# A hybrid encoder layer on one core: 16 more tokens by gathered expert rows, activations weighted and split for two expert blocks at a time

## The chip, the cores and the metric

The kernel runs on one core of a Trainium2 chip. The metric is the device time of one execution in microseconds, as the median of several runs. The engines of the core work side by side and are tied by semaphores: TensorE (PE, matrix products; its weight loads are shown as PEld), VectorE (DVE), ScalarE (ACT), GpSimd (POOL, which here mostly issues gathers) and SyncE (SP, which issues the other transfers, in order).

## The reference

One layer of an encoder over 512 tokens of width 1024. An RMSNorm and one input projection feed an attention branch and a bidirectional state-space branch (S5, followed by a gated linear unit); both are gated, merged and projected out. Then comes the part that takes most of the time, a layer of 16384 single-neuron experts: each token has 8 heads, each head picks 16 experts by product keys (two lists of 128 keys), and the token's output is the gated sum over its 128 experts. A last RMSNorm ends it.

```python
def peer(h, w_query, sub_keys, w_down, w_up):
    ...
    scores = jnp.einsum('thnd,hnkd->thnk', q, sub_keys).astype(jnp.float32)
    s_top, i_top = lax.top_k(scores, PEER_TOPK)
    ...
    best, pos = lax.top_k(cand, PEER_TOPK)
    idx = jnp.take_along_axis(cand_idx, pos, axis=-1)
    gate = jax.nn.softmax(best, axis=-1)
    ...
    u = w_down[ib]
    act = jax.nn.gelu(jnp.einsum('cd,chkd->chk', xb, u).astype(jnp.float32)) * gb
    v = w_up[ib]
    return jnp.einsum('chk,chkd->cd', act.astype(v.dtype), v)
```

## The kernel before

**Numbers.** fp32 weights and activations are split into two fp16 halves (hi and lo), and a product is three fp16 matmuls: hi·hi, lo·hi, hi·lo. ACT makes the hi half of a weight tile, DVE the lo half (`halves`, L453 and L456 for experts; `Stream.hi` and `Stream.lo`, L485 and L493, for the other weights). `Stream` loads the other weights in a fixed order into three raw buffers (`wr`), each 128x1024.

**Front.** ACT squares the eight 128x512 pieces of x (L694). After each, four fp32 matmuls with a single column add its squares over the partitions (L696). Four square roots (L700), a reciprocal (L703) and a spread over partitions (L563, L572) lead to the first normed piece (`h_of`, L710) and the first projection (`pu`, L725 to L727). Then follow the S5 branch, attention, and from about 288 to 345 us the attention projection (`w_oa`), the GLU (`w_glu`) and the S5 output (`w_os`), whose weights come through `Stream`.

**Experts.** Two ways are used for the experts. Of the 512 tokens, 384 (tiles 1 to 3) are dense: every expert is computed for them, in 128 blocks of 128 experts. `ph1(i)` is the down projection of block i: 24 matmuls of 384 columns (L541 to L543) into a bank, then the gelu on ACT (L1479) into a slot of 128x384. There are 13 slots in the memory `area` and 35 in a ring. `ph2(i)` is the up projection: DVE multiplies the slot with the block's gates `Gb` (L1501), ACT rounds the product to fp16 `ph` (L1502), DVE makes the rest `pl` (L1503), and 18 matmuls of 512 columns (L1514 to L1516) add to six PSUM sums `ya` (three token tiles by two halves of the width). The other 128 tokens (tile 0) are gathered: for each of their 128 experts an indirect DMA fetches one row of `w_down` per token (128 rows of 4 KB), DVE reduces it against h (`gdown`, L1552), and later a row of `w_up` is weighted and added (`gup`, L1560). These are 256 gathers on ten row buffers.

**Gates.** Before ph2 the dense tokens' gates must stand as a matrix over experts. The one-hot stage makes it in 24 subtiles of 16 tokens: DVE builds one-hot factors (`ej` L1427, `eg` L1429 and L1431), PE multiplies them (L1442), ACT copies the result into a staging tile `stg` (L1444), and every 64 tokens 4 MB go to DRAM (`gd`). `gload` reads a block's gates back, 192 KB in pieces of 64 floats.

**Order.** `experts()` lists units and runs them in a row. The ph1 units come first while slots last (between the top-k of tiles 1 to 3, and within the one-hot stage), then ph2(0) and so on, with one ph1 between two ph2 while there are any, and at the end only ph2. The weights of a unit are prepared three units ahead. At the start of the pair part DVE does the top-k of tile 0. After that `gather_init` fills the list of gathers, and a planner paces them: `tp` adds up PE's cost of the units, `td` DVE's cost, and while `td` is less than `E.lead` ahead and `room` allows (it grows by `E.gcap` = 1.42 per unit), one row is worked off and one more is fetched (L1545). What is left ten units before the end is done at once. Then follow the last sums, final norm and store.

## Time and profile before

| | before |
|---|---|
| median of 3 runs | 1563.29 us (1563.12 to 1567.69) |
| profiled execution: its own time | 1559.74 us |
| profiled execution: span | 1558.0 us, 26141 instructions |
| PE busy | 1502.0 us (96%), 9921 matmuls |
| DVE busy | 1296.7 us (83%) |
| ACT busy | 742.9 us (48%) |
| POOL busy | 374.5 us (24%) |
| moved | 378.64 MB, mean 243 GB/s |

The span runs from the first to the last instruction; the execution's own time is a little longer. Busy shares are means over stages that have different limits, so a stretch is looked at by itself: first which engine is busy throughout in it, then what the others wait for. A matmul's own duration overlaps the next one's, so the distance from start to start is what one costs. "Engine time" of transfers is time on the core's 16 DMA engines; a share of 1.00 or more means that all 16 had something in hand.

### The profile page before, as it was taken

To read this page: it belongs to the slowest core of one execution; us is meant where nothing else is said; L and a number is where in the kernel's file an instruction comes from. 1 tells how busy PE (TensorE), PEld (TensorE's weight loads), DVE (VectorE), ACT (ScalarE), POOL (GpSimd) and SP (SyncE) were. 2 spreads that over 40 slices of the span, in tenths; PEclk is the share of its full clock that TensorE was granted. 3 is DMA by queue.
4 is the path that set the end of the run, shared out by engine and by line. 5 is a ranking of instruction groups with operands and counts; after the bars stand their busy time and mean duration, and the time that the engine had idled before them with its cause. 6 is when DMAs were issued, how large, how long until landed. Compare 5 with 4: busy or idle time off the path is not lost. (4 is left out here: it accounts for less than half of the span.)

```text
span 1558.0 us, 26141 instructions
## 1 busy us (share of the span) xinstructions
PE 1502.0 (96%) x9921; PEld 854.9 (55%) x9921; DVE 1296.7 (83%) x2571; ACT 742.9 (48%) x1117; POOL 374.5 (24%) x300
## 2 busy tenths in 40 slices
PE   8999999889989999999999999999999999999997
PEld 5547665448676567664444555555555555554433
DVE  4889688555999999986987988888888888888886
ACT  5456765554345479883432443333333333333334
POOL 0100100000000000000026654444555445444310
PEclk9999999999999999999999999999999999999999
DMA  5532622764103347769669999999999999999984
GB/s 192 129 97 49 94 69 90 238 201 157 42 15 125 125 140 284 277 252 332 177 218 389 385 385 366 349 347 348 367 344 354 348 345 368 351 311 323 324 270 147
DMA packets 201135, 378.64 MB, mean 243 GB/s; under 512 B 112305, under 2 KB 117809, under 8 KB 199985
## 3 DMA queue, kind: packets, MB, share of 16 engines
q1 hardware_dynamic: 159904, 231.50, 44.5%
q0 software_dynamic: 39520, 142.59, 26.9%
q10 hardware_dynamic: 1584, 2.88, 0.6%
q8 instruction: 77, 1.26, 0.3%
q14 instruction: 50, 0.40, 0.1%
HBM read 340.25 MB, written 36.14 MB: 242 GB/s over the span
## 5 line engine op out<-in xcount | busy, mean ns | idle before, releaser
L456 DVE SCALAR_TENSOR_TENSOR wlo<-raw,whi 128x1024 f16<-128x1024 f32 x256 | 311.9, 1220 | 125.3 <-ACT whi L453 124.2
L453 ACT ACTIVATE whi<-raw 128x1024 f16<-128x1024 f32 x256 | 262.0, 1050 | 168.7 <-DMA raw<-w_up 94.6
L1514 PE MATMUL ya<-whi,ph 128*128 128x512 f16 x768 | 291.9, 380 | 8.1 <-ACT ph L1502 6.1
L1515 PE MATMUL ya<-wlo,ph 128*128 128x512 f16 x768 | 291.8, 380 | 2.9 <-DVE wlo L456 2.6
L1516 PE MATMUL ya<-whi,pl 128*128 128x512 f16 x768 | 291.8, 380 | 1.0
L1545 POOL DMA_INDIRECT row<-w_dn,gidx x78 | 104.7, 1342 | 625.4 <-ACT whi L453 537.2
L543 PEld LDWEIGHTS <-wlo 128*128 128x128 f16 x1272 | 124.6, 98 | 111.7 <-DVE wlo L493 9.9
L541 PEld LDWEIGHTS <-whi 128*128 128x128 f16 x1272 | 124.6, 98 | 105.1 <-ACT whi L485 11.3
L542 PEld LDWEIGHTS <-whi 128*128 128x128 f16 x1272 | 124.6, 98 | 91.3 <-issue 1.3
L1502 ACT ACTIVATE ph<-Gb 128x384 f16<-128x384 f32 x128 | 66.5, 520 | 214.9 <-DVE Gb L1501 195.7
L1545 POOL DMA_INDIRECT row<-w_up,gidx x78 | 107.5, 1378 | 122.0 <-DVE area L1560 96.5
L1516 PEld LDWEIGHTS <-pl 128*128 128x128 f16 x768 | 75.3, 98 | 101.3 <-DVE pl L1503 11.7
L541 PE MATMUL rps<-hhl,whi 128*128 128x384 f16 x384 | 125.6, 327 | 2.6 <-ACT whi L453 2.6
L543 PE MATMUL rps<-hhl,wlo 128*128 128x384 f16 x384 | 125.9, 328 | 2.0 <-DVE wlo L456 2.0
L1514 PEld LDWEIGHTS <-ph 128*128 128x128 f16 x768 | 75.3, 98 | 94.4 <-ACT ph L1502 10.2
L542 PE MATMUL rps<-hhl,whi 128*128 128x384 f16 x384 | 125.6, 327 | 0.0
L1515 PEld LDWEIGHTS <-ph 128*128 128x128 f16 x768 | 75.3, 98 | 87.7 <-issue 2.6
L1444 ACT COPY stg<-rps 128x512 f32<-128x512 f32 x96 | 98.3, 1077 | 16.4 <-PE rps L1442 15.7
L543 PE MATMUL rota<-hhl,wlo 128*128 128x384 f16 x320 | 104.3, 326 | 1.4 <-DVE wlo L456 1.4
L541 PE MATMUL rota<-hhl,whi 128*128 128x384 f16 x320 | 104.3, 326 | 0.0
L542 PE MATMUL rota<-hhl,whi 128*128 128x384 f16 x320 | 104.3, 326 | 0.0
L541 PE MATMUL rotb<-hhl,whi 128*128 128x384 f16 x320 | 104.3, 326 | 0.0
(370 smaller groups left out, 2994.4 us busy)
## 6 DMA issues: line engine op xcount, KB each, us to landing
raw<-w_dnT SPq DMA_DIRECT2D x128, 512.0 KB
raw<-w_up SPq DMA_DIRECT2D x128, 512.0 KB
gd<-stg SPq DMA_DIRECT2D x6, 4096.0 KB
Gb<-gd SPq DMA_DIRECT2D x128, 192.0 KB
raw<-w_g SPq DMA_DIRECT2D x16, 512.0 KB
raw<-w_out SPq DMA_DIRECT2D x8, 512.0 KB
raw<-w_query SPq DMA_DIRECT2D x8, 512.0 KB
x<-x SPq DMA_DIRECT2D x8, 512.0 KB
```

The source lines that it names most:

```text
L453: E.nc.scalar.activation(hi, raw, AF.Copy, scale=scale)
L456: E.nc.vector.scalar_tensor_tensor(lo, raw, scale, hi, op0=OP.mult, op1=OP.subtract)
L541: E.nc.tensor.matmul(o, lhsT=lh, rhs=rh, start=start and i == 0, stop=False)
L542: E.nc.tensor.matmul(o, lhsT=lh, rhs=rl, start=False, stop=False)
L543: E.nc.tensor.matmul(o, lhsT=ll, rhs=rh, start=False, stop=stop and i == n - 1)
L1444: nc.scalar.copy(self.stg[:, :, t0:t0 + TQ].rearrange("p i t -> p t i"), o)
L1502: hi, lo = halves(E, wp, raw, D, "up", 3, SU, lambda: nc.scalar.activation(ph, P, AF.Copy, scale=scale))
L1514: nc.tensor.matmul(o, lhsT=ph[:, ts], rhs=hi[:, ns], start=f, stop=False)
L1515: nc.tensor.matmul(o, lhsT=ph[:, ts], rhs=lo[:, ns], start=False, stop=False)
L1516: nc.tensor.matmul(o, lhsT=pl[:, ts], rhs=hi[:, ns], start=False, stop=l)
L1545: E.nc.gpsimd.indirect_dma_start(out=r, out_offset=None, in_=E.a[src], in_offset=bass.IndirectOffsetOnAxis(ap=E.gidx[:, k:k + 1], axis=0))
```

## The change

1. **16 tokens more by gathers.** Of the 384 dense tokens the last 16 are gathered instead (`TX`, `TN` = 368). ph1's matmuls and the gelu cover 368 columns; the last 16 columns of the slots are zeroed once by GpSimd, so that ph2 still covers 384. The one-hot stage has 23 subtiles. The 16 tokens have 128 experts each, 2048 rows; they are laid on 128 partitions as 16 tokens by 8 heads, with 16 experts each. So they take 16 more gathers per weight (32 in all, 288 instead of 256). Their results (`yx`) are summed over the 8 partitions of a token by two fp32 matmuls with `sel` that add to `ya` (`extra`).
2. **Two blocks at a time.** The slots and the gates come in pairs: the product, the rounding to fp16 and the remainder are made once per two blocks of 384 (at even ph2 units), and a gate load brings two blocks (384 KB in pieces of 128 floats).
3. **Buffers and pace.** Eight row buffers instead of ten (`NX` = 4), a ring of 17 pairs and 6 pairs in `area` (46 slots instead of 48). The planner's numbers change: a ph1 unit costs DVE 1.25 instead of 1.14, a ph2 unit 3.15 or 1.25 instead of 2.2, a row 1.29 instead of 1.2, and `E.gcap` is 1.68.
4. **Front.** DVE adds the squares, then four matmuls instead of 32, one square root instead of four; the hi halves of the first two weight tiles stand ahead of the root.
5. **Wider weight buffer.** From the attention projection's stage to the end of `w_os`, `Stream` has seven raw buffers in memory that the S5 part has left.

```diff
+TX = 16
...
+    def widen(self, pool, last):
+
+        self.wide, self.end = pool, self.at[last] + 1
...
-            r = self.pool.tile([128, 1024], F32, name="raw", tag="wraw", bufs=self.bufs)
+            pool, bufs = (self.wide, 7) if i < self.end else (self.pool, self.bufs)
+            r = pool.tile([128, 1024], F32, name="raw", tag="wraw", bufs=bufs)
...
-            sso = [ps.tile([128, 1], F32, name="pss", tag="ps") for _ in range(4)]
             for k in range(KT):
                 nc.scalar.activation(sq[:, k], xT[:, k], AF.Square)
-                for c in range(4):
-                    nc.tensor.matmul(sso[c], lhsT=sq[:, k, c * 128:c * 128 + 128], rhs=E.ones[:, 0:1],
-                                     start=(k == 0), stop=(k == KT - 1))
+                if k:
+                    V.tensor_add(sq[:, 0], sq[:, 0], sq[:, k])
+            sso = ps.tile([128, 4], F32, name="pss", tag="ps")
+            for c in range(4):
+                nc.tensor.matmul(sso[:, c:c + 1], lhsT=sq[:, 0, c * 128:c * 128 + 128], rhs=E.ones[:, 0:1],
+                                 start=True, stop=True)
+            st.hi()
+            st.hi()
...
+            nc.scalar.activation(ssx, sso, AF.Sqrt, scale=1.0 / D, bias=E.eps)
...
+            w2c = ExitStack()
+            st.widen(w2c.enter_context(E.pool(name="w2", bufs=1)), "os7")
...
     TD = T - 128
+    TN = TD - TX
...
-    NX = 6
+    NX = 4
...
+        for x in self.ring:
+            self.E.nc.gpsimd.memset(x[:, :, self.TN:], 0.0)
+        self.E.nc.gpsimd.memset(self.area, 0.0)
...
+        E.dma(self.xi, E.xidx.rearrange("a (r s) -> (a r) s", s=16))
+        E.dma(self.xg, E.xgate.rearrange("a (r s) -> (a r) s", s=16))
+        E.dma(self.hx, E.xh[:, None, :].to_broadcast([TX, 8, D]))
+        E.dma(self.sel, E.a["sel"])
...
-            P = self.G[i]
-            V.tensor_tensor(P, self.slot(i), P, op=OP.mult)
-            hi, lo = halves(E, wp, raw, D, "up", 3, SU, lambda: nc.scalar.activation(ph, P, AF.Copy, scale=scale))
-            V.scalar_tensor_tensor(pl, P, scale, ph, op0=OP.mult, op1=OP.subtract)
+            if i % 2:
+                hi, lo = halves(E, wp, raw, D, "up", 3, SU)
+            else:
+                G, R = self.G[i // 2], self.pair(i // 2)
...
+                V.tensor_tensor(byc(R), byc(R), G, op=OP.mult)
+                hi, lo = halves(E, wp, raw, D, "up", 3, SU,
+                                lambda: nc.scalar.activation(self.ph, R, AF.Copy, scale=scale))
+                V.scalar_tensor_tensor(self.pl, R, scale, self.ph, op0=OP.mult, op1=OP.subtract)
...
+    def extra(self):
+
+        for n in range(2):
+            ns = slice(n * 512, n * 512 + 512)
+            self.E.nc.tensor.matmul(self.ya[2][n], lhsT=self.sel, rhs=self.yx[:, ns], start=False, stop=False)
...
-    E.lead, E.gcap = 1.0, 1.42
+    E.lead, E.gcap = 1.0, 1.68
```

How the program's order of instructions changes is shown at three places. The first is DVE at the very start, before:

```order
L1869 MEMSET ones 128x128
L1871 MEMSET eps 128x1
L703 RECIPROCAL ssx<-ssx 128x4
L563 TENSOR_TENSOR dgs<-ident,ssx 128x512
L493 SCALAR_TENSOR_TENSOR wlo<-raw,whi 128x1024
```

and after:

```order
L1930 MEMSET ones 128x128
L1932 MEMSET eps 128x1
L705 TENSOR_TENSOR sqx<-sqx 128x512 x7
L713 RECIPROCAL ssx<-ssx 128x4
L573 TENSOR_TENSOR dgs<-ident,ssx 128x512
L503 SCALAR_TENSOR_TENSOR wlo<-raw,whi 128x1024
```

The seven adds of the squares now stand on DVE ahead of the reciprocal; they are what PE's 28 further sums were.

The second is SP's queue of loads for the attention projection's stage (`w_oa`, with `w_out` and `w_query` for later stages between them), before:

```order
L1860 DMA raw<-w_out 128x1024
L1860 DMA raw<-w_oa 128x512
L1860 DMA raw<-w_query 128x1024
L1860 DMA raw<-w_oa 128x512
L1860 DMA raw<-w_query 128x1024
L1860 DMA raw<-w_oa 128x512
```

and after:

```order
L1921 DMA raw<-w_query 128x1024 x4
L1921 DMA raw<-w_oa 128x512
L1921 DMA raw<-w_query 128x1024
L1921 DMA raw<-w_oa 128x512
L1921 DMA raw<-w_glu 128x512 x2
```

With more buffers open, four loads of `w_query` come in a row ahead of the last two of `w_oa`, and `w_glu` follows at once.

The third is DVE in the pair part, before (the `ISA` rows are `gdown` and the reading of its sum; `area,gco` is `gup`):

```order
L1560 SCALAR_TENSOR_TENSOR area<-area,gco 128x1024
L1501 TENSOR_TENSOR Gb<-ring_5625,Gb 128x384
L456 SCALAR_TENSOR_TENSOR wlo<-raw,whi 128x1024
L1503 SCALAR_TENSOR_TENSOR pl<-Gb,ph 128x384
L1552 ISA area,gact<-area,h_2654 128x1024
L1552 ISA gact 128x1
L1560 SCALAR_TENSOR_TENSOR area<-area,gco 128x1024
L456 SCALAR_TENSOR_TENSOR wlo<-raw,whi 128x1024
L1552 ISA row_8331,gact<-row_8331,h_2654 128x1024
L1552 ISA gact 128x1
L1501 TENSOR_TENSOR Gb<-ring_5626,Gb 128x384
```

and after:

```order
L1549 TENSOR_TENSOR ring_5601<-ring_5601,Gb 128x6x2x64
L460 SCALAR_TENSOR_TENSOR wlo<-raw,whi 128x1024
L1552 SCALAR_TENSOR_TENSOR pl<-ring_5601,ph 128x768
L460 SCALAR_TENSOR_TENSOR wlo<-raw,whi 128x1024
L1614 SCALAR_TENSOR_TENSOR yx<-row_8210,gco,yx 128x1024
L1606 ISA area,gact<-area,h_2630 128x1024
L1606 ISA gact 128x1
L460 SCALAR_TENSOR_TENSOR wlo<-raw,whi 128x1024
L1614 SCALAR_TENSOR_TENSOR yx<-area,gco,yx 128x1024
L1606 ISA area,gact<-area,h_2630 128x1024
L1606 ISA gact 128x1
L460 SCALAR_TENSOR_TENSOR wlo<-raw,whi 128x1024
```

The product and the remainder are now of twice the width and come once in four `wlo` instead of once in two; between two `wlo` stand up to two steps of gathered rows.

## Rows read from the trace of the kernel before

**Rows 1.** The page: busy us (share of the span) and instructions by engine.
```profile
PE 1502.0 (96%) x9921; PEld 854.9 (55%) x9921; DVE 1296.7 (83%) x2571; ACT 742.9 (48%) x1117; POOL 374.5 (24%) x300
```

**Rows 2.** Timeline of the front (start, duration, instruction), and a 128x512 add.
```profile
8.40 3.30 ACT L694 ACTIVATE sqx<-xTs 128x512 f32<-128x512 f32 x5 [1.48 <-DMA xTs<-xT]
...
18.59 0.18 DVE L703 RECIPROCAL ssx<-ssx 128x4 f32<-128x4 f32 x1 [17.56 <-ACT ssx L700]
...
11.71 6.54 PE L696 MATMUL pss<-ones,sqx 128*128 128x1 f32 x30
...
L1267 DVE TENSOR_TENSOR zm<-zm,mixed 128x512 f32<-128x512 f32 x8 | 5.5, 692 | 0.3
```

**Rows 3.** Busy by engine, clock, DMA share, GB/s; then waits (total, times, longest).
```profile
288.00:345.00 57.00, 46.62 (x195) 17.72 (x194) 33.40 (x45) 30.14 (x47) 0.00 (x0) 0.97 0.67 208
...
PE pp L541 <- ACT whi L485: 6.4, 6, 2.0
```

**Rows 4.** Timeline of DVE, one period of the one-hot stage.
```profile
599.60 2.48 DVE L1431 TENSOR_TENSOR eg<-eg,ghl 128x2048 f16<-128x2048 f16 x2
602.01 1.22 DVE L456 SCALAR_TENSOR_TENSOR wlo<-raw,whi 128x1024 f16<-128x1024 f32 x1
603.14 1.22 DVE L1427 TENSOR_TENSOR ej<-iom,gij 128x2048 f16<-128x2048 f16 x1
...
605.53 2.48 DVE L1431 TENSOR_TENSOR eg<-eg,ghl 128x2048 f16<-128x2048 f16 x2
```

**Rows 5.** Timeline of PE, one pair: 24 matmuls of ph1, 18 of ph2.
```profile
1004.16 0.33 PE L541 MATMUL rota<-hhl,whi 128*128 128x384 f16 x1
...
1008.06 0.38 PE L1514 MATMUL ya<-whi,ph 128*128 128x512 f16 x1
...
1011.95 0.33 PE L541 MATMUL rotb<-hhl,whi 128*128 128x384 f16 x1
```

**Rows 6.** Busy of PE, PEld, DVE, ACT, POOL by stretch, clock, DMA share, GB/s.
```profile
860.00:1000.00 140.00, 140.00 (x757) 73.90 (x756) 124.88 (x159) 54.02 (x75) 77.62 (x54) 1.00 1.04 372
1000.00:1400.00 400.00, 400.00 (x2158) 211.01 (x2157) 341.39 (x430) 150.79 (x212) 198.73 (x147) 1.00 1.00 349
1405.00:1551.00 146.00, 139.94 (x632) 60.16 (x630) 120.88 (x163) 56.13 (x84) 34.88 (x27) 1.00 0.85 272
```

**Rows 7.** Chain that ended last, burst and tail: start, duration, what.
```profile
828.60 19.57 DMA raw<-w_up
...
1432.41 7.20 DMA raw<-w_up
```

**Rows 8.** Groups by line (count, busy, mean ns): a clear on GpSimd, the fp32 scores.
```profile
masks.py:197 POOL MEMSET ident<- 128x128 f32 x1 | 0.2, 206 | 0.3 <-POOLq L1898 0.3
...
L911 PE MATMUL pS<-KT,QT 96*128 96x512 f32 x64 | 33.2, 641 | 0.7 <-ACT KT L897 0.7
```

**Rows 9.** Timeline of DVE in the pairs (start, duration, instruction).
```profile
855.70 1.28 DVE L1560 SCALAR_TENSOR_TENSOR area<-area,gco 128x1024 f32<-128x1024 f32 x1
856.90 0.55 DVE L1501 TENSOR_TENSOR Gb<-ring,Gb 128x384 f32<-128x384 f32 x1
857.37 1.21 DVE L456 SCALAR_TENSOR_TENSOR wlo<-raw,whi 128x1024 f16<-128x1024 f32 x1
```

**Rows 10.** Transfers: 860 to 920, then 1000 to 1200, then 1420 to 1500.
```profile
DMA packets 12454, 23.07 MB, mean 385 GB/s; under 512 B 7234, under 2 KB 7234, under 8 KB 12449
...
DMA packets 37974, 70.33 MB, mean 352 GB/s; under 512 B 22065, under 2 KB 22065, under 8 KB 37960
...
q0 software_dynamic: 10508, 38.25, 53.4%
q1 hardware_dynamic: 27452, 31.90, 46.4%
...
DMA packets 19768, 26.14 MB, mean 327 GB/s; under 512 B 14227, under 2 KB 14227, under 8 KB 19762
...
q1 hardware_dynamic: 16315, 13.52, 52.7%
```

## What the change does to the time: the prediction

> **What bounds the kernel now.** First the page's busy shares [rows 1]: TensorE (PE) is busy 96% of the span, VectorE (DVE) 83%. So time can be won where PE has less to do, or in the few stretches in which it waits. A table of busy time by stretch, laid over the stages, then tells who sets the pace of each:
> - first norm: the reciprocal starts at 18.59, 6.9 after the last square, and everything waits for it [rows 2];
> - 288 to 345 (attention projection, GLU, S5 output): PE works 46.62 of 57 us; its waits end on the ACT half-split of weights that arrive by `Stream` [rows 3];
> - one-hot stage, 550 to 696: DVE works without a gap, a period of 5.93 us [rows 4];
> - pairs of a ph1 and a ph2 unit, 860 to 1405: PE is 100% busy, DVE 85 to 89%, the transfer engines at a share of 1.00 to 1.04 [rows 5, 6]. This is a third of the kernel;
> - gather burst, around 804 to 860: ten gathers go out at once, and one load of weights takes 19.57 us [rows 7];
> - tail, 1405 to 1551: only ph2; loads of w_up take 7 us and more of the chain behind gathered rows [rows 6, 7].
>
> **Front.** Before, ACT's squares end at 11.70, but PE's 64 records of sums (32 fp32 matmuls of one column, two records each; the last 30 take from 11.71 to 18.25) go on, and four square roots wait for them, one behind the other [rows 2]. Now DVE adds the squares as they come, seven adds of 0.69 (the 128x512 add of [rows 2]), about the 0.66 between two squares, so the last ends near 12.6. Four sums of one column remain, eight records, 0.22 apart by 6.54/30: 14.3. A root over 4 columns, 0.3 as other small steps, then the reciprocal starts at 14.7 instead of 18.59: **−3.9**. The two half-splits of u0 and u1 now stand ahead of the root on ACT; the squares end at 11.70, so they fit beside PE's sums if their weights have landed, which the order of the loads suggests. Bounds −2 to −4.5.
>
> **Wider weight buffer.** From the time the S5 memory is free (284 to 288) until os7 the stream holds seven raw buffers instead of three. That takes away nothing but waits for transfers. PE is idle 10.4 of the 57 us, 6.4 of it in waits for ACT's half-split, six times [rows 3]; the rest are dependencies (sigmoid, mixing) that stay. The DMA share there is 0.67, so there is room to load ahead. I take **−6**, with 0 and −10.4 as ends. What speaks against: SP issues in order, and three w_query loads now stand ahead of the last two w_oa loads; if w_oa then comes late, ACT waits for it as before.
>
> **Token index copies, memsets.** topk of tile 3 gets one more DVE instruction of 128 wide; its copies to DRAM are off the path. GpSimd clears the rings and the area. Its memset of 128x128 took 0.206 [rows 8]; if that is all columns, 5120 of them and 17 clears of 32 are 9 us, and less if a fixed part is in it. If ACT's first gelu waits for that it does so while DVE sets the pace. **+0.3**, end +4.
>
> **One-hot stage.** 23 subtiles of 16 tokens instead of 24. A subtile is, on DVE, two compares (1.14 each) and two products (2.48 for both): 4.80 from one to the next without the wlo of 1.13 that belongs to the ph1 unit beside it [rows 4]. n1 falls from 48 to 46, so two units' wlo leave as well: 4.80 + 2×1.13 = 7.06. **−7.0**, as long as DVE sets the pace. The two ph1 units come back in the pair part.
>
> **Transition.** Before the first ph2, SP gets four loads (indices, gates, a 512 KB broadcast of h, sel) ahead of Gb and w_up, but Gb comes in pairs in 512-byte instead of 256-byte pieces. +1 and −2; I take **−1**, ends −3 and +3.
>
> **Pairs: PE.** A 384-column matmul starts 0.1625 after the one before (24 take 3.90 us), a 512-column one 0.216 after (18 take 3.89): 7.79 a pair [rows 5]. 368 columns are no row of before; the nearest are 384 and 512, which both give 0.42 ns a column, so 0.1557 is an estimate and a ph1 unit 3.74. ph2 stays, as its 18 matmuls cover 128 tokens whether or not 16 are zero. The two units moved here cost 2×3.74: **+7.5**. The other 80 pairs: 7.63 at PE's pace, −0.16 each, −12.8 in all, if DVE and transfers allow it. The two extra fp32 matmuls of 512 columns, two records each, are like the fp32 scores, whose records are busy 0.641 each, overlap and all [rows 8]: at most 2.6, of which I take two thirds: **+1.7**.
>
> **Pairs: DVE.** Before: two wlo (1.13 by [rows 4]), P and pl (0.47 each, 384 wide) and 2.82 gathered rows (up to 1.20) [rows 9], 2.26+0.94+3.38 = 6.58; the row of 1000 to 1400 gives 341/400×7.79 = 6.65 [rows 6]. After: P and pl come once for two blocks, 768 wide. By the line from 384 (0.55 busy) to 1024 (1.21) that is 0.95, so 0.87 for each pair of units instead of 0.94; the four-dimensional order of P is seen in no row, end: twice 0.47, no gain. The gathered rows rise to 288 in all, paced at 13 per 8 units: 3.25 a pair, 3.90 us. Sum 7.03 of 7.63, or 92%. From 860 to 1000 DVE was busy 124.88 of 140 us, 89%, with PE at 140.00 [rows 6], so 92% is likely affordable. But each wlo that PE needs stands behind up to one row more.
>
> **Pairs: transfers.** A pair moves 524 KB for w_dnT, 524 for w_up, 197 of Gb and 524 per gathered row: before 1.245+2.82×0.524 = 2.72 MB, in 7.79 us 350 GB/s, which is just what the row of 1000 to 1400 shows (349). So there the need sets the rate. After: 1.245+3.25×0.524 = 2.95 MB; in 7.63 us 386 GB/s. From 860 to 920 the chip moved 23.07 MB, 385 GB/s, with 256-byte Gb pieces [rows 10] and with PE busy throughout [rows 6]. At that rate a pair takes 7.66: **−10.4** for 80 pairs (80×0.13). If only the steady 352 of [rows 10] were to be had, 2.95/0.352 = 8.38, +0.75 a pair against PE's pace. The engines' time says how tight it is. Let q1's 256-byte packets take a each and its large ones b a MB: the 200 us from 1000 give 22065a + 26.25b = 0.464×16×200, the 80 us from 1420 give 14227a + 9.88b = 0.527×16×80 [rows 10]; so a is 19.5 ns and b 40 us. A gathered row takes 23.4 us of engines' time (53.4% of 3200 us for 38.25 MB). After, a pair needs 42 for weights, 384 pieces of Gb at 19.5 to 39 ns, 7.5 to 15, and 3.25×23.4 = 76: 126 to 133 us on 16 engines, 7.9 to 8.3 at a share of 1.00. At the share of 1.04 that stood from 860 to 1000 [rows 6] it is 7.6 to 8.0. I take 7.66, the value of the rate that was seen while PE was not held back.
>
> The Trainium skill (page "DMA: Bandwidth & Descriptors", section "Specifications") puts the HBM limit of one NeuronCore at about 358 GB/s: by it a pair could not be under 2.95/0.358 = 8.24 us, and the change would lose about 36 us on the 80 pairs (an estimate from that page's figure). The trace disagrees: 385 GB/s for 60 us. The same section names 512 B as the least transfer at line rate; by it the Gb pieces would leave the slow kind and stand at the low end, which no run here shows yet.
>
> **Burst and tail.** Eight row buffers instead of ten let fewer gathers run ahead, but they are asked for faster: **0**, −5 to +3 by what a longer or shorter wait of that 19.57 us [rows 7] could do. In the tail PE does 630×0.216 = 136 us of work in 146: 10 lost, mostly waits for w_up [rows 6, 7]. It asks for 10 rows per 8 units instead of 11.4 and for Gb in half the packets. By the same a and b (21 us for weights, 15 for Gb before and 7.5 to 15 after, 11.4/8 rows of 23.4 before and 10/8 after) a unit's time on 16 engines falls from 4.3 to between 3.6 and 4.1, against PE's 3.9: **−4**, ends 0 and −8.
>
> **Sum.** −3.9 −6 +0.3 −7 −1 +7.5 +1.7 −10.4 +0 −4 = −22.8; I take back 2 for PE's waits on a fuller DVE: −20.8. Against the profiled execution's own 1559.74 (span 1558.0): 1538.9. The median is 1563.29, 0.23% above it, and the forecast of the median is 1563.29/1559.74×1538.9 = 1542.5.
>
> **Rivals.**
> - B, the pairs stay where they were: DVE's and the transfers' fuller queues hold a pair near 7.79. The −10.4 is gone: about 1553. For it: shares over 1.00. Against: PE at 140.00 of 140 from 860 to 1000.
> - D, the wide buffer and the earlier roots bring nothing: w_oa comes behind w_query on SP, and the clears on GpSimd hold up the first gelus. −6 and −3 or so gone, +2 more: about 1554. For it: ACT's waits there are for several tensors; against: a DMA share of 0.67.
> - C, slower: the transfers cannot go above the steady 352 GB/s over hundreds of us (HBM reads of scattered rows), and a pair takes 8.38 instead of 7.66: 80×0.72 = 58 us more, about 1600. It decides from a pair of 7.92 us, that is 372 GB/s, where the whole gain of 20.8 is spent. The limit on the Trainium skill's page above would make this case the true one. Against it: 385 GB/s from 860 to 920, and 372 from 860 to 1000 with PE at 140.00 of 140 [rows 6, 10].
>
> **How the numbers follow.** Forecast 0.58, B 0.17, D 0.15, C 0.10. Forecast's own range, from the ends of its terms: 1528 to 1552. The range reaches to B and D with some of their own width: 1528 to 1562, and leaves out C and a little. Within 0.3% (1558.6 to 1568.0; about what a measurement here tells from no change) lie the worse ends of B and D: 0.07. Slower is C: 0.10. Faster 0.83.
>
> **What would show it.** Reciprocal near 14.7; PE busy over 50 of 55 us in the oa stage; 23 subtiles at 5.93; ph1 matmuls 0.156 apart; pairs at 7.66 with a rate near 385 GB/s and PE busy throughout. I am wrong if PE has waits for w_up or w_dnT all through the pairs (C), or if matmuls of 368 columns start as far apart as those of 384 (then −10.4 is gone).

## The result, and the profile after

| | before | after |
|---|---|---|
| median | 1564.32 us (4 runs) | 1547.59 us (1544.27 to 1549.59, 4 runs) |
| ratio | | 0.9887, 95% interval 0.9864 to 0.9911 |
| profiled execution, span | 1558.0 us | 1545.6 us |

The changed kernel is faster by 1.1%, 16.7 us in the medians. The forecast was 1542.5, its own range 1528 to 1552. The time came out 5 us above the forecast, but the way to it was another one: two terms failed, a third was mis-sized, the pairs gave more than forecast, and one number that the change does not touch turned out to be worth as much as the whole change (the third buffer, below).

The page of the changed kernel, first lines (busy us, share of the span, instructions):

```profile
span 1545.6 us, 25606 instructions
...
PE 1472.6 (95%) x9837; PEld 844.0 (55%) x9837; DVE 1330.7 (86%) x2496; ACT 724.8 (47%) x1047; POOL 461.3 (30%) x352
```

Against [rows 1], PE has 29 us less to do and the span is 12.4 shorter: PE waits more than before. Where, is read by laying both timelines beside each other. The table takes the start of the first or last instruction of a kind in both traces and the difference between them; a step in the last column is what that stretch gave.

| mark | before | after | difference | step |
|---|---|---|---|---|
| last gate projection matmul (`pg`) | 288.15 | 284.03 | −4.1 | −4.1 |
| first `w_query` matmul | 380.17 | 371.22 | −8.9 | −4.8 |
| first one-hot `ej` | 549.82 | 545.72 | −4.1 | **+4.8** |
| last `stg` copy | 695.48 | 684.60 | −10.9 | −6.8 |
| first ph1 matmul of the pairs | 777.82 | 765.76 | −12.1 | −1.2 |
| last ph1 matmul of the pairs | 1404.94 | 1392.86 | −12.1 | 0.0 |
| last ph2 matmul | 1550.89 | 1538.41 | −12.5 | −0.4 |

Two ph1 and two ph2 units more lie between the marks of the pairs (82 and 81 instead of 80 and 79), one ph2 unit less before them and one less behind.

The marks are of one trace each, and a step moves by itself from trace to trace. From the last `pg` to the first `w_query` matmul the ten traces with the changed code there took 84.4 to 89.8 us (87.2 in the table's), those with the old code 92.0 and 93.1. The one-hot stage repeats within 0.1 us. The tail took 141.8 to 145.6 us in the five traces with the same code there; the table has the longest of them.

The front, timeline (start, duration, instruction):

```profile
7.45 2.64 ACT L703 ACTIVATE sqx<-xTs 128x512 f32<-128x512 f32 x4 [1.33 <-DMA xTs<-xT]
...
8.12 3.88 DVE L705 TENSOR_TENSOR sqx<-sqx 128x512 f32<-128x512 f32 x5 [1.27 <-ACT sqx L703]
14.25 0.18 DVE L713 RECIPROCAL ssx<-ssx 128x4 f32<-128x4 f32 x1 [2.25 <-ACT ssx L712]
...
13.95 0.26 ACT L712 ACTIVATE ssx<-pss,eps 128x4 f32<-128x4 f32 x1 [1.23 <-PE pss L708]
14.12 1.05 ACT L495 ACTIVATE u1hi<-raw 128x1024 f16<-128x1024 f32 x1
...
12.05 1.87 PE L708 MATMUL pss<-ones,sqx 128*128 128x1 f32 x8 [12.05 <-DVE sqx L705]
```

The adds follow the squares, four sums take 1.87 and the reciprocal starts at 14.25 instead of 18.59 [rows 2]. Of the two half-splits that the section on the change puts ahead of the root, only the first stands there (at 11.67): the kernel has one `st.hi()` in that place, not two, and the second (`u1hi`) follows the root.

PE in one pair, timeline:

```profile
1015.65 0.32 PE L551 MATMUL rota<-hhl,whi 128*128 128x368 f16 x1
1015.81 0.32 PE L552 MATMUL rota<-hhl,whi 128*128 128x368 f16 x1
...
1019.39 0.38 PE L1564 MATMUL ya<-whi,ph 128*128 128x512 f16 x1
...
1023.28 0.32 PE L551 MATMUL rotb<-hhl,whi 128*128 128x368 f16 x1
```

A pair takes 7.63 instead of 7.79 [rows 5]; 24 matmuls of 368 columns take 3.74. From 893.65 on every pair takes just that: PE sets the pace. The stretches answer to [rows 6] (busy of PE, PEld, DVE, ACT, POOL, then clock, DMA share, GB/s):

```profile
860.00:1000.00 140.00, 140.00 (x771) 75.13 (x770) 132.85 (x152) 52.89 (x68) 89.79 (x61) 1.00 1.04 397
1000.00:1400.00 400.00, 400.00 (x2202) 215.23 (x2201) 368.62 (x417) 148.31 (x188) 255.46 (x170) 1.00 1.02 388
1393.00:1539.00 146.00, 139.01 (x618) 60.64 (x615) 114.26 (x125) 52.20 (x68) 38.31 (x25) 0.98 0.77 261
```

The transfers run at 388 to 397 GB/s over 540 us, DVE is busy 92 to 95%, and PE does not wait in them. In the tail it does: 612 matmuls of ph2 instead of 630, and the same 146 us.

### The profile page after: what moved, and what is told of

Its sections match the earlier page's. It is cut to its first block, busy times and chain, and to the rows that moved or that the text cites. A ratio compares the mean times of both kernels' runs of the same rounds, so it can differ in the third digit from the quotient of the medians.

```text
span 1545.6 us, 25606 instructions
## 1 busy us (share of the span) xinstructions
PE 1472.6 (95%) x9837; PEld 844.0 (55%) x9837; DVE 1330.7 (86%) x2496; ACT 724.8 (47%) x1047; POOL 461.3 (30%) x352
## 4 chain that ended last, share of the span: by engine, by line
PE 54%; DVE 22%; issue 11%; DMA 8%; ACT 4%; POOL 1%; SPq 0%; ACTq 0%; DVEq 0%; POOLq 0%
PE ya L1566 6%; PE ya L1564 6%; PE ya L1565 6%; DMA raw<-w_up 5%; DVE wlo L460 4%; PE rotb L552 3%; PE rota L552 3%; PE rota L551 3%; PE rotb L551 3%; PE rotb L553 3%; PE rota L553 3%; PE pg L551 1%; PE pg L552 1%; PE pg L553 1%; PE pp L553 1%
## 5 line engine op out<-in xcount | busy, mean ns | idle before, releaser
L457 ACT ACTIVATE whi<-raw 128x1024 f16<-128x1024 f32 x256 | 265.4, 1050 | 288.4 <-DMA raw<-w_up 219.6
L1599 POOL DMA_INDIRECT row<-w_dn,gidx x64 | 87.5, 1368 | 160.7 <-DVE gidx L1157 111.8
L553 PE MATMUL rps<-hhl,wlo 128*128 128x368 f16 x368 | 119.2, 324 | 7.4 <-DVE wlo L460 7.0
L1599 POOL DMA_INDIRECT area<-w_up,gidx x64 | 105.0, 1640 | 66.9 <-DVE area L1614 50.0
L551 PE MATMUL rps<-hhl,whi 128*128 128x368 f16 x368 | 118.8, 323 | 1.9 <-ACT whi L457 1.9
L552 PE MATMUL rps<-hhl,whi 128*128 128x368 f16 x368 | 118.7, 323 | 0.0
L552 PE MATMUL rotb<-hhl,whi 128*128 128x368 f16 x328 | 104.8, 320 | 0.0
L551 PE MATMUL rotb<-hhl,whi 128*128 128x368 f16 x328 | 104.8, 319 | 0.0
L552 PE MATMUL rota<-hhl,whi 128*128 128x368 f16 x328 | 104.8, 319 | 0.0
L553 PE MATMUL rotb<-hhl,wlo 128*128 128x368 f16 x328 | 104.8, 319 | 0.0
L551 PE MATMUL rota<-hhl,whi 128*128 128x368 f16 x328 | 104.8, 319 | 0.0
```

The lines of the kernel that those rows point to most:

```text
L457: E.nc.scalar.activation(hi, raw, AF.Copy, scale=scale)
L551: E.nc.tensor.matmul(o, lhsT=lh, rhs=rh, start=start and i == 0, stop=False)
L552: E.nc.tensor.matmul(o, lhsT=lh, rhs=rl, start=False, stop=False)
L553: E.nc.tensor.matmul(o, lhsT=ll, rhs=rh, start=False, stop=stop and i == n - 1)
L1599: E.nc.gpsimd.indirect_dma_start(out=r, out_offset=None, in_=E.a[src], in_offset=bass.IndirectOffsetOnAxis(ap=s[1][:, k % 128:k % 128 + 1] ...
```

## Experiments

Each group of runs had runs of the kernel before beside it, whose median lay between 1562.24 and 1565.50. The changed kernel was timed beside the first group only (1564.32). So a difference of medians to the changed kernel is good to about 3 us; the ratio to the kernel before of the same group, given in brackets with its 95% interval, is the safer measure, and where a cause is to be found the traces decide. The changed kernel's own ratio is 0.9887 (0.9864 to 0.9911).

### What holds the top-k up: the clears on GpSimd

Between the first `w_query` matmul and the one-hot stage 4.8 us of the lead were lost, with DVE busy throughout. Summed by instruction, one group of DVE had grown by 5.04 us, the CAST of the top-k's positions. Its four instructions in the kernel before, and in the kernel after (count, busy, mean ns):

```profile
L1115 DVE CAST pf<-pi 128x640 f16<-128x640 uint16 x4 | 1.3, 328 | 0.1
```

```profile
L1127 DVE CAST pf<-pi 128x640 f16<-128x640 uint16 x4 | 6.4, 1588 | 0.1
```

Timeline of GpSimd and DVE after:

```profile
467.21 1.03 POOL L1406 MEMSET ring<- 128x32 f32 x16 [2.62 <-PE rps L1375]
468.18 4.37 POOL L1407 MEMSET area<- 128x5120 f32 x1
...
467.35 5.38 DVE L1127 CAST pf<-pi 128x640 f16<-128x640 uint16 x1
```

Three casts took 0.33. The fourth began among GpSimd's clears and ended 0.18 us after the last of them.

**The small clear.**

```diff
-        self.E.nc.gpsimd.memset(self.area, 0.0)
...
+        for x in self.first:
+            self.E.nc.gpsimd.memset(x[:, :, self.TN:], 0.0)
```

> The changed kernel, but GpSimd clears only the last 16 columns of the 12 slots in the area (192 columns) instead of all 5120. In the changed kernel DVE's CAST of 128x640 took 5.38 us where its three siblings took 0.33, and it ended 0.18 us after the end of GpSimd's 4.37 us clear. Theory (the clear holds the cast off): the cast takes 0.33 to 0.5, the one-hot stage starts about 5 us earlier, the whole is 4.5 to 5.5 us shorter than the changed kernel, about 1542.5. Rival (the cast waits for something else in its place of the program, and the clear is beside it by chance): the cast stays at about 5.4 and the time at about 1547.5.

Measured: 1541.64 (0.9863, 0.9835 to 0.9891), 5.95 under the changed kernel's median, about 4 by the ratios, whose intervals overlap. The cast:

```profile
466.68 1.44 DVE L1127 CAST pf<-pi 128x640 f16<-128x640 uint16 x1
```

It still waits for the small clears, which end at 467.94, again 0.18 before it; the stretch lost 1.0 us instead of 4.8. The rival falls: what holds the cast is the clears. The cast did not come down to the 0.33 to 0.5 that was expected, and not all of the gain is the cast's: the profiled span is 7.7 us shorter, 3.8 of it in this stretch and 3.7 in the tail, for which the clear gives no reason.

**Two clears.** The clear of the area is written twice.

> The changed kernel with the area cleared twice in a row by GpSimd. Theory (the cast is held until the clear of the area ends): if the second clear follows without letting the cast in, the cast takes about 9.8 us and the whole is 4.4 longer, about 1552; if the cast gets in between the two, it stays near 5.4 and the second clear costs nothing. Rival (a slower rate while both run, not a hold): the cast would grow by less than a clear's length, 0.3 to 2 us.

Timeline of GpSimd, then DVE:

```profile
471.21 4.37 POOL L1407 MEMSET area<- 128x5120 f32 x1
475.64 4.43 POOL L1408 MEMSET area<- 128x5120 f32 x1
...
470.38 5.38 DVE L1127 CAST pf<-pi 128x640 f16<-128x640 uint16 x1
```

The cast ends at 475.76, behind the first large clear, and the second costs the cast nothing: it is a hold, not a slower rate. The hold is not for one instruction only: the cast stood through the row of small clears and the large one behind it, and got in only then. The single execution took 1550.85; its top-k stretch lost 4.3 us. A third case came by chance in the run of the late loads below, whose cast started before the row of clears and was not held:

```profile
467.67 1.03 POOL L1406 MEMSET ring<- 128x32 f32 x16 [2.62 <-PE rps L1375]
468.64 4.37 POOL L1407 MEMSET area<- 128x5120 f32 x1
...
466.19 0.33 DVE L1127 CAST pf<-pi 128x640 f16<-128x640 uint16 x1
```

So the price of this clear depends on where the cast falls: 5 us or nothing. All traces agree: where the large clear stands, the cast took 5.37 to 5.38 in five and 0.33 in the one above; with the small clears 1.44 in two and 0.33 in one, where it again came ahead of the row; without clears, in five traces, always 0.33. From the first `w_query` matmul to the one-hot stage it is 173.9 to 175.9 us where the cast was held by the large clear, and 169.0 to 170.7 in all others.

### The transition

PE stood before the second token tile of the first ph2 unit. The timeline of PE there:

```profile
710.04 0.38 PE L1566 MATMUL ya<-whi,pl 128*128 128x512 f16 x1
714.87 0.38 PE L1564 MATMUL ya<-whi,ph 128*128 128x512 f16 x1 [4.45 <-ACT ring L1523]
```

and of ACT:

```profile
712.67 1.06 ACT L457 ACTIVATE whi<-raw 128x1024 f16<-128x1024 f32 x1 [2.44 <-DMA raw<-w_up]
713.63 0.83 ACT L1551 ACTIVATE ph<-area 128x768 f16<-128x768 f32 x1
714.36 0.46 ACT L1523 ACTIVATE ring<-rps 128x368 f32<-128x368 f32 x1
```

The sum's bank is free only after the last gelu of the old banks; on ACT that gelu stands behind a half-split that waits for a w_up load. In the kernel before, the same wait was 1.86 us, ahead of the first tile.

**Late loads.** The four loads of the 16 tokens (`xi`, `xg`, `hx`, `sel`) move from `main` to `gather_init`.

> The changed kernel, but the four loads for the 16 tokens (indices, gates, the 512 KB of h, sel) are issued when the gathers begin instead of ahead of the first w_up and Gb loads. In the changed kernel PE stood 4.83 us before the second token tile of the first ph2 unit and then ran at the lower clock for about 4 us; the transfers were at a share of 1.04 there. Theory (0.6 MB ahead of w_up at 350 GB/s): the first w_up issues 4 to 8 us earlier, the wait before the second tile of ph2 shrinks by 1.5 to 4 us, and the whole by as much, 1544 to 1546. Rival (ACT's order sets that wait: the last gelu stands behind the hi half of a later w_up): the wait stays at 4 to 5 us and only moves, the gain is 1.5 at most.

Measured: 1542.26 (1535.09 to 1544.14; 0.9866, 0.9839 to 0.9893). In the profiled run, from the last `stg` copy to the first ph1 of the pairs, 4.9 us less than in the changed kernel, and PE's wait for the gelu is 1.5. But the first 16 pairs then take 130.1 instead of 127.9: about half the gain is given back. (In this execution, of 1535.09 us, the cast was free too, so its time alone says little about the loads.)

**Both.** The small clear, and the loads five units behind the first ph2.

> The changed kernel with the small clear (192 columns of the area instead of 5120) and with the four loads for the 16 tokens issued five units after the first ph2 unit, while DVE does the top-k of tile 0 and the transfers' share is 0.5 to 0.8, ahead of the gathers. Theory (held cast 4 to 5 us and loads in a full queue 2 to 5 us are two separate losses, and the loads cost nothing in the quiet stretch): the sum of both, 6 to 10 us under the changed kernel, 1537 to 1541, and the first 8 pairs no longer than with the loads ahead. Rival (one makes good for the other, as PE waits for the transfers at the transition anyway): as the small clear alone, 1541 to 1543.

Measured: 1540.25 (0.9860, 0.9844 to 0.9877). The transition is 4.6 us shorter than in the changed kernel, the pairs to their last ph1 matmul 3.7 us longer, and the first 8 pairs took 8.75 each instead of 8.19, against the theory. Beside the small clear alone the loads' place is worth 1.4 us by the medians, not 2 to 5: mostly the rival. (The cast, too, was free here by its place.)

Where the gain goes can be read from the traces. The second and fourth pair take 8.43 and 8.67 instead of 7.62: PE comes earlier, and its waits there end on DVE's `pl` and `wlo`, while DVE still does the top-k of tile 0. The fifth takes 14.7 instead of 12.2. That pair is long in every run, before (10.2) and after: DVE, in its order, stands for the first gathered row, and a `wlo` that PE needs stands behind it. In the changed kernel, DVE and PE:

```profile
800.66 1.23 DVE L1606 CUSTOM_DVE_ANT_0 row<-row,h 128x1024 f32<-128x1024 f32 x1 [4.20 <-DMA row<-w_dn,gidx]
...
801.81 1.22 DVE L460 SCALAR_TENSOR_TENSOR wlo<-raw,whi 128x1024 f16<-128x1024 f32 x1
...
803.08 0.38 PE L1565 MATMUL ya<-wlo,ph 128*128 128x512 f16 x1 [2.70 <-DVE wlo L460]
```

### The pairs: how near the transfers' limit is

**Small pieces.** The gate load of two blocks is made as two loads.

```diff
-            self.E.dma(g.rearrange("p c b t -> p c (b t)"), ...)
+            for b in range(2):
+                self.E.dma(g[:, :, b], self.E.gd.rearrange("c j i t -> j c i t")[:, :, 2 * len(self.G) + b])
```

> The changed kernel, but each gate load of two blocks is made as two loads in pieces of 256 bytes instead of one in pieces of 512; bytes, rows and DVE's work are the same. Theory (a 256-byte packet costs 19.5 ns of engine time, so a pair needs 133 us on 16 engines): pairs go from 7.625 to between 7.9 and 8.3 us, the rate falls below 375 GB/s, the whole is 20 to 55 us longer, 1568 to 1602, slower than the kernel before if it is over 1568. Rival (the pairs hold their pace whatever the pieces, as PE sets it): 7.63, and the time within 3 us of 1547.5.

Measured: 1558.51 (0.9971, 0.9956 to 0.9986), 10.9 above the changed kernel. In 900 to 1380, the changed kernel first, then the small pieces:

```profile
DMA packets 73210, 188.13 MB, mean 392 GB/s; under 512 B 5856, under 2 KB 30432, under 8 KB 73175
...
q1 hardware_dynamic: 43250, 78.73, 44.6%
```

```profile
DMA packets 96131, 184.76 MB, mean 385 GB/s; under 512 B 54094, under 2 KB 54094, under 8 KB 96096
...
q1 hardware_dynamic: 66904, 78.01, 47.6%
```

Neither side was right on the size. In means of eight, pairs take 7.63 to 7.79 (8.69 in the burst), 6 us more from the first ph1 to the last, and the tail takes 3 more. Taken by size, the packets of these two windows last 28.7 ns on average for a piece of 512 B and 18.4 ns for one of 256 B (the prediction's sum gave 19.5), and those of 4 KB take 41 us a MB. So larger pieces save a fifth of a gate load's engine time, 384 times 8 ns or 0.2 us a pair on 16 engines. That is little, but the pairs stand so near the limit that it decides. (The number of gate loads doubles too; its part was not separated.)

**More rows.** `E.gcap` 1.9 and 1.15 for a row.

> The changed kernel with the planner's limit raised (1.9 instead of 1.68 a unit, a row costed at 1.15 instead of 1.29), so that about 3.5 to 3.7 gathered rows go into a pair instead of 3.25 and few are left for the tail. A pair then moves 3.1 to 3.2 MB; at PE's 7.625 us that is 407 to 417 GB/s. Theory (transfers end at about 385 to 400 GB/s, as the share of 1.02 to 1.05 in both kernels suggests, and DVE has 98% to do): pairs go to 7.75 to 8.1, 10 to 35 us over 82 pairs, and the tail gives back up to 9: 1549 to 1575. Rival (the rate still follows the need, and the tail's loss came from its rows): pairs stay at 7.63, the tail is 6 to 9 us shorter, 1539 to 1542.

Measured: 1553.01 (0.9943, 0.9920 to 0.9966). The stretch from 900 to 1380, with the changed kernel's below it:

```profile
900.00:1380.00 480.00, 472.40 (x2579) 251.43 (x2577) 448.85 (x514) 171.82 (x224) 312.12 (x216) 1.00 1.04 397
```

```profile
900.00:1380.00 480.00, 480.00 (x2646) 258.65 (x2645) 447.93 (x508) 180.80 (x231) 309.94 (x207) 1.00 1.03 392
```

The rate stops at 397 GB/s and PE waits; pairs take 7.63 to 8.16 in means of eight, 13.9 us more over the pairs, while the tail is 8.2 shorter. The theory holds. The chain behind PE's waits runs through loads of w_up of 12 to 15 us, so the two buffers of the section on the tail could be thought the cause instead of a limit. More rows with three buffers were not run; but no run moved more than 399 GB/s over any 200 us, also not those with three buffers, and no run with pieces of 256 B more than 386. The changed kernel's pace of 1.68 lies just under the limit.

### Parts alone

**The front** on the kernel before.

> The kernel before with only the new front (DVE adds the squares, four sums, one root, the two hi halves ahead of it). Theory (the gain of the first 20 us is kept to the end, since PE or DVE is busy throughout behind it): first projection at 18.8 instead of 23.3 and the whole 3.5 to 4.5 shorter than before, 1560. Rival (it is given back at a later wait for transfers, such as the S5 stage's or the weights'): first projection as early, the whole 0 to 1.5 shorter.

Measured: 1561.92 against 1562.24 (0.9994, 0.9971 to 1.0017). The lead is 3.3 us at the last gate projection, 1.3 at the first `w_query` matmul, 1.9 at the end of the one-hot stage, 0.2 at the last ph1 before the pairs, and nothing at the end. This speaks for the rival, but the interval reaches from 4.5 us of gain to 2.7 of loss and does not exclude the theory's lower end. Where `w_oa` and `w_glu` are loaded, PE's wait for ACT's half-splits grew from 6.4 to 8.6 us, about what the lead lost there; that it is always lost so is not shown.

**The wide buffer** on the kernel before (`widen`, `load` and `lo` as in the change).

> The kernel before with only the seven raw buffers for the attention projection's stage. Theory (the waits there are for loads that start too late): from the end of the gates' projection to the first w_query matmul 4 to 6 us shorter, the whole as much, 1558 to 1560. Rival D of the prediction (w_oa comes behind w_query on SP, nothing is won): within 1.5 us of before in that stretch and in the whole.

Measured: 1558.43 against 1562.24 (0.9967, 0.9951 to 0.9983), 5.8 us ahead at the first `w_query` matmul. The theory holds: the stretch itself is 6.3 us shorter, the whole 2.7 to 7.7 by the interval. Together with the front the lead there is 8.9 in the changed kernel, more than 1.3 + 5.8. But it is 5.4 to 12.4 in the ten traces with both, so whether the two help each other is not shown.

**Pairing alone,** without the 16 tokens.

> The changed kernel without the gathered 16 tokens: 384 dense tokens, 24 subtiles, 256 gathers at the old pace (1.42), no clears, no four loads, no closing sums; front, wide buffer, pairing of blocks, 46 slots and eight row buffers as in the changed kernel. Theory (the 16 tokens are worth their own terms: 4.8 for a subtile and 82 times 0.16 for the pairs, less 1.7 for the closing sums, 5 for the held cast and 4 at the transition): pairs at 7.785, one-hot stage longer by 4.8, no held cast, the whole 1551 to 1555. Rival (the lower need for transfers, 2.72 MB a pair, gives more at the burst and the tail than the 16 tokens bring): 1544 to 1549.

Measured: 1552.80 (0.9934, 0.9909 to 0.9958), pairs of 7.785, no held cast, the one-hot stage 4.9 longer from first to last `ej`. So the 16 gathered tokens are worth 5.2 us of the 16.7 by the medians, about 7 by the ratios; the theory's sum of their terms is 7.2.

### The tail

The tail did not get shorter. The chain that ended last in the changed kernel shows a cycle of 17.5 us for four ph2 units, which PE does in 15.5:

```profile
1464.84 7.49 DMA raw<-w_up
...
1475.53 1.28 DVE area L1614
...
1480.38 0.95 DVE ring L1549
1481.33 1.18 DVE wlo L460
1482.51 0.02 issue
1482.53 7.39 DMA raw<-w_up
```

The load starts when DVE has made the lo half before it, which frees one of the two raw buffers, and DVE makes that behind gathered rows.

**A third buffer for w_up.**

```diff
-    E.wb = (3, 2)
+    E.wb = (3, 3)
```

> The changed kernel with three raw buffers for w_up instead of two; nothing else. In its tail a chain repeats every 17.5 us for four ph2 units that PE does in 15.5: load of w_up 7.2 to 7.5, hi half, lo half, pl, gathered rows on DVE, lo half, and only then the next load. Theory (the load is late because its buffer comes free late): with a third buffer the chain breaks, the tail of 145.5 us gets 3 to 7 shorter, the whole 1541 to 1545. Rival (the transfers' rate with rows and gates among them is the limit, or DVE's work): tail within 2 us of 145.5, the whole within 3 of 1547.6.

Measured: 1539.47 (0.9854, 0.9838 to 0.9871). The tail takes 134.6 us instead of 145.5; its work is 34×18×0.216 + 1.7 for the closing sums = 133.9. What ACT's half-split waited for most, in the changed kernel and with three buffers (total, times, longest):

```profile
ACT whi L457 <- DMA raw<-w_up: 65.5, 16, 6.9
```

```profile
ACT whi L457 <- PE ya L1566: 53.3, 27, 3.5
```

Loads no longer come late; ACT waits for PE, as it should. The theory was right in kind and too small by 4: 10.9 us are far outside the 141.8 to 145.6 that the tail took with two buffers. The first 8 pairs take 8.64 instead of 8.19 each (DVE's wait for the first gathered row is 6.8 us instead of 4.2), the second 8 are at 7.63 instead of 7.79; together 2.2 us were given back.

**On the kernel before,** the same one number.

> The kernel before with three raw buffers for w_up instead of two; nothing else. In it the tail took 145.96 us for 136 us of matmuls. Theory (the two buffers, not the packets of the gate loads or the gathered rows, set the tail's loss in the kernel before too): tail 136 to 139, the whole 6 to 9 us shorter than before, 1553 to 1557, unless the burst takes some of it back. Rival (the step of the prediction: the engines' time of 4.3 us a unit with 256-byte gate pieces sets it): tail within 3 us of 146, the whole within 3 of before.

Measured: 1548.82 against 1565.50 (0.9896, 0.9880 to 0.9913). The tail is 136.0 instead of 146.0, and the burst is shorter too: the second 8 pairs take 7.82 instead of 8.53, 5.6 us. (The trace reaches the pairs 4.6 us later than that of the kernel before, so the two spans differ by 11.0 only.) From 1396, and in the burst:

```profile
1396.00:1537.00 141.00, 141.00 (x661) 64.43 (x660) 125.41 (x167) 58.03 (x83) 42.30 (x30) 1.00 0.89 292
```

```profile
804.00:860.00 56.00, 54.03 (x291) 28.22 (x290) 46.33 (x72) 18.09 (x27) 39.45 (x29) 1.00 0.99 360
```

With 256-byte pieces and rows at 292 GB/s the tail runs without a wait. The theory holds, the rival falls. The third buffer alone brings as much as the whole change.

**All three** (small clear, loads in the quiet stretch, third buffer) on the changed kernel.

> The small clear, the four loads in the quiet stretch and the third raw buffer for w_up together on the changed kernel. Theory (three separate losses): the sum of what the two other runs of this call win against 1547.6, 1532 to 1538. Rival (earlier w_up loads only take the place of rows and gates in the same transfers): as the first two alone, 1537 to 1541.

Measured: 1530.05 (0.9792, 0.9775 to 0.9808), 17.5 under the changed kernel and the fastest of all. The sum of 7.3 and 8.1 was 15.4 (by the ratios it is 15 against 4 and 5), so the rival falls, and the gain is 2 us beyond the theory's range. A part of the surplus shows in the trace: with the third buffer the second and fourth pair are back at 7.62, so what the loads' place gains at the transition is no longer lost there. With the small clears the cast took 1.44.

## Why the prediction was right, point by point

The sum was −20.8; the profiled spans differ by −12.4, the medians by −16.7, since the profiled run of before took 1559.74, 4.6 under its median.

- **Front, −3.9.** Measured −4.3 at the reciprocal and −4.1 at the last gate projection. Right for the place, with one half-split ahead of the root instead of the two that it speaks of; that the gain is kept to the end was not argued, and alone none of it was left at the end of the trace.
- **Wide buffer, −6.** Measured −4.8, alone −6.3 in the stretch; −2.2 to −7.6 in the ten traces with it. The size was right within what a trace tells. Rival D falls for the buffer (w_query ahead of w_oa did no harm); its other half, that the clears on GpSimd cost something, came true, but through DVE and not through the gelus.
- **Copies and clears, +0.3 with an end of +4.** Measured +4.8. This step failed. The clear's length was bounded well (4.37), but the prediction looked for who waits for its data, the gelu, and not for what else GpSimd can hold up: DVE's cast stood for 5.38 us until 0.18 after the clear. The Trainium skill has a reason for it (page "SBUF — State Buffer", section "Who interferes with whom"): casts can run in a mode that takes the port pair that VectorE shares with GpSimd, and the one that comes second stands until the other's instruction has ended. The traces agree with the stand-still; that the port pair is its cause no run here shows, and through a row of small clears the cast stood longer than one instruction.
- **One-hot stage, −7.0.** Measured −6.8, DVE's period unchanged at 5.92.
- **Transition, −1.** Measured +2.7 like for like (−1.2 with one ph2 unit of 3.9 fewer). The step counted the loads' own time; it missed that a gelu on ACT behind a late w_up holds PE's sums (4.45 us of idle PE instead of 1.86). Right after that wait the granted clock fell from 1.0 to 0.5, from 2.4 to 1.2 GHz, for 3.4 us from 715.24 on, and the matmuls came 0.43 apart instead of 0.22. The four loads are not the only cause: in the kernel before with a third buffer, which has none of them, the wait was 4.43.
- **Pairs, 7.66 a pair.** Measured 7.63, PE's own pace, at the 388 to 397 GB/s that the row of 860 to 920 had promised. Rivals B and C fall. The Trainium skill's limit of 358 GB/s (page "DMA: Bandwidth & Descriptors", section "Specifications") would have made C true; the trace shows 388 to 397, and the measurement decides. The Trainium skill's row works that figure out as half of what a stack gives to two cores; this kernel ran on one, and no run here shows what a second one would change. The 2 us taken back for DVE were not needed. Step by step for pairs and burst together: +6.9 was forecast with the units that moved (7.5 + 7.8 − 10.4 + 2), 0.0 came. Of these 6.9, 2.4 are the pace of 7.63, 2 the DVE term, and 2.5 the burst, which the prediction put at 0 with −5 to +3: the first 16 pairs took 8.4 us over the pace before and 5.9 after. Why the burst got shorter was not tested: other traces have 6.1 and 8.0 with the old code there, 6.1 and 6.4 with the changed one, so a part of it is luck.
- **Closing sums, +1.7.** Four records 0.43 apart (128x512 fp32): 1.7. Right.
- **Tail, −4.** Measured +1.8 like for like (−0.4, with 3.9 for one unit less and 1.7 for the sums). This step failed by its reason: the loss was laid to the engines' time a unit, and it was the order in which two buffers come free (a third one took the tail to 136.0 with the old pieces). Part of the +1.8 is the clock: in the changed kernel's tail the granted clock fell to 0.5 (1.2 GHz) twice for 3.4 us, at 1476.41 and 1513.96, each time after waits of PE, and in the kernel before not at all. That costs about 3.4 us (an estimate: half of the two stretches), so the waits themselves shrank by about 1.6, and in the four other traces with the same code the tail is 0.3 to 3.8 us shorter. The sign of the term can be defended, its size and its reason cannot. The row of the first fall (busy of PE, PEld, DVE, ACT, POOL, then clock, DMA share, GB/s):

```profile
1474.00:1482.00 8.00, 7.09 (x24) 2.71 (x25) 7.96 (x8) 2.86 (x4) 3.96 (x3) 0.79 0.87 306
```

The tail's mean share of 0.85 [rows 6] does not tell the reason either. The mean takes in a last part with little to move; where most of PE's idle time lies in the kernel before, the share is 0.90 to 0.99 at 285 to 320 GB/s (1448 to 1512, in steps of 16 us), while with three buffers its transfers reached 349 to 369 (1436 to 1500). What tells it is the chain: each load of w_up starts just behind the lo half that frees its buffer.

The misses of +4.5, +3.7, +5.8 and +1.2 (the wide buffer) stand against 6.9 that the pairs and the burst gave beyond the forecast; that leaves the 8 us by which the spans missed it. The medians missed it by 4 us only because the kernel before ran faster than its median while it was profiled. The time was right in part because errors of both signs met.

## What to carry to other kernels

Where loads come late, look in the chain for what each load waits for, here the lo half that frees its buffer, before counting bytes; the third buffer was one number. An instruction on an engine that nobody waits for can still hold up another engine's (the cast: 5.38 us instead of 0.33), so clear only what must be zero. A gain at the front of a chain can be lost at the next stage that waits. And before a step of a few us is read from one trace, see how far it moves in traces with the same code.

## What the runs showed of the hardware

- A DVE cast of 128x640 from uint16 to f16, 0.33 us alone, was held for as long as GpSimd cleared memory: 1.44 us by a row of small clears, 5.38 by the row's rest and a large one behind it; between two large clears it got in. DVE's two f16 products of the one-hot stage were not held by a GpSimd clear beside them (2.49 us, 2.48 without):

```profile
660.75 1.80 POOL L1478 MEMSET stg<- 128x2048 f32 x1 [188.20 <-DVE eg L1469]
...
660.69 2.49 DVE L1471 TENSOR_TENSOR eg<-eg,ghl 128x2048 f16<-128x2048 f16 x2
```

- One core moved 397 GB/s over 480 us, 59% of it in gathered rows, at a share of 1.04. More was not to be had with more asked for; over 200 us no run here moved more than 399 (386 with pieces of 256 B).
- A piece of 512 B took 29 ns of engine time and one of 256 B 18 ns; packets of 4 KB moved 512 B in 21 ns. The Trainium skill (page "DMA: Bandwidth & Descriptors", section "Specifications") names 512 B as the least transfer at line rate, which the prediction took as its low end; here such a piece is still well short of the large packets' rate.
